# Two-layer decoder trunk: round-trip loads, splits, scores and products issued later, two output chunks interleaved, and some transposes moved from TensorE to VectorE and DMA

## The chip, the cores and the metric

The kernel runs on one core of one Trainium2 chip. The metric is the device time of one execution in microseconds. Before the change it is 958.38 us, the median of three runs (958.22 to 959.68).

## The reference, cut to what matters

`x` is 256 tokens by 2048, in fp32. Layer 0 has eight heads A (a mixture of three dilated windows, computed here as one softmax with counts folded into a mask) and four heads B (differential attention with values of 256). Layer 1 has sixteen causal heads. Both layers have the same shape:

```python
h  = rmsnorm(x, norm) @ w_in                 # 2048 -> 8192 columns: q, k, v and the gate z
ya = softmax(rope(q) rope(k)^T + mask) v     # 24 heads in all
yb = rmsnorm((softmax(q1 k1^T) - lam * softmax(q2 k2^T)) v, subln) * (1 - lam_init)   # heads B
y  = concat(ya, yb) * silu(z)
x  = x + y @ w_out                           # 2048 -> 2048
```

After layer 1 a last rmsnorm follows.

## The kernel before

**Weights set the pace.** Each layer has 20 chunks of 512 weight columns, sixteen of `w_in` and four of `w_out`. A chunk is 16 slots, one for each 128 rows of the weights; the program has 640 slots. In a slot TensorE runs six matmuls of 128x512: two halves of the tokens, and for each three products (`mm3`) of high and low parts, since each fp32 operand is split into two float32r parts whose sum it is. Weights come by DMA (`raw`), ScalarE copies the high part (`wh`, line 123) and VectorE subtracts for the low part (`wl`, line 124), two slots per instruction. The split of slot s is written three such pairs ahead (`AHEAD`), into four buffers.

**Order of chunks.** Layer by layer `v0 q0 k0 z0`, then `q k z v` of groups 1, 2 and 3, then `o0` to `o3` of the output. A group has four heads; groups 2 and 3 of layer 0 have two heads B each, which use two scores per head.

**Work beside the slots** is hung on slots with `at(slot, function)`; it is emitted after the matmuls of that slot. The scheduler below the program may put an instruction earlier on the queue of an engine when it thinks it ready, and engines run their queues in order. With `nxt` for the slot after a chunk's end:

- `evac_rope` (lines 260 to 270, at nxt and nxt+1) turns a chunk of q or k by the rotary tables on VectorE; `evac_z` makes the gate. Both end in `turn`, which brings the token-major 128x512 result into head-dimension-major form: a 32x32-block transpose on VectorE (`bz`, line 240), a store to DRAM (`dt`, line 242) and four loads per half, each of 32 partitions (line 248). All these DMAs are issued by GpSimd's queue, POOL, in its order; each takes it some time, and an issue waits at the head of the queue for what it needs.
- `split_rope` (nxt+18) splits q and k into high and low (`qh`, `kh` on ScalarE, line 279; `ql`, `kl` on VectorE, line 280).
- `first` is nxt of k plus 22 (20 in group 3). `attn_s` for head h at first+3h: scores (`ps_s`) and softmax into `p`. `attn_t` at first+3+3h: transpose of `p` by the same round trip (`bt`, `d`, loads at line 354). `attn_h` at first+15+3h (13 in group 3): splits into `th` (ScalarE, line 363) and `tl` (VectorE). `attn_o` two slots later: the product with v on TensorE (`po`), then `finish_y`, which multiplies by the gate and splits y into `yh`, `yl`.
- Heads B: `diff_s` twice, `attn_t`, `attn_h` at first+15+5h, `diff_o` a slot later (`pdo`; then squares, a power on GpSimd and `yb`), and `diff_y` at first+20+4h: four TensorE transposes of `yb` (line 416) and `finish_y`.
- An output chunk ends in `evac_o` (x plus the product); in layer 0 `next_x` at nxt+3 and nxt+6 makes the next layer's x by eight TensorE transposes per chunk (line 433) and `split_x`.

## Time and profile before

| | |
|---|---|
| median of three runs | 958.38 us |
| the profiled execution | 960.44 us, of which its span on the core 958.7 us |
| TensorE (PE), matmuls | 931.4 us busy, 97% of the span, 4282 instructions |
| VectorE (DVE) | 646.2 us, 67% |
| ScalarE (ACT) | 467.5 us, 49% |
| GpSimd (POOL), DMA issues above all | 214.8 us, 22% |
| DMA engines | 213 MB, 222 GB/s |
| mean granted TensorE clock | 0.991 |

Matmuls overlap, so the duration of one is not what it adds to the path. That is the distance from its start to the start of the next, which the timeline shows. An idle stretch of TensorE stands in brackets before the instruction that ended it, with what released it.

### The profile page before, as it was taken

The numbers are of one execution on the slowest core, as the hardware profiler recorded it, in microseconds if no ns is written. First come the engines' busy times: TensorE is split into PE (matmuls) and PEld (weight loads), VectorE is DVE, ScalarE is ACT, GpSimd is POOL, SyncE is SP. The second block draws the span as 40 slices with busy tenths as digits, with TensorE's granted clock in tenths as the row PEclk, the third lists the DMA queues.
The fourth block names the chain that finished last, engine by engine and source line by source line (L and its number), as shares of the span: only waits on it lengthen the run. The fifth ranks groups of instructions, "written<-read, shape, count | busy, mean of one in ns | idle before, by whom it ended". The sixth has DMA issues, their size and how long they took to land. (4 is left out here: it accounts for less than half of the span.)

```text
span 958.7 us, 11998 instructions
## 1 busy us (share of the span) xinstructions
PE 931.4 (97%) x4282; PEld 773.0 (81%) x4282; DVE 646.2 (67%) x1002; ACT 467.5 (49%) x705; POOL 214.8 (22%) x392
## 2 busy tenths in 40 slices
PE   9999997999999999999999999989999999999996
PEld 7888876888888888878888888768888888887886
DVE  6675876677667767665554667767677767786572
ACT  7533643554355446445454345445534554455450
POOL 0012343242223222200000223522422332251000
PEclk9999998999999999999999999999999999999999
DMA  8785765676666666545555757766666666677542
GB/s 335 257 321 209 248 233 183 237 254 213 230 219 229 215 245 207 196 166 182 194 195 177 249 191 271 239 201 236 237 219 238 247 231 228 220 246 259 179 173 88
DMA packets 43644, 213.22 MB, mean 222 GB/s; under 512 B 9472, under 2 KB 11008, under 8 KB 23488
## 3 DMA queue, kind: packets, MB, share of 16 engines
q1 hardware_dynamic: 27360, 174.55, 52.3%
q0 software_dynamic: 15360, 36.20, 11.4%
q10 hardware_dynamic: 864, 1.70, 0.5%
q8 instruction: 33, 0.54, 0.2%
q14 instruction: 27, 0.22, 0.1%
HBM read 192.23 MB, written 20.19 MB: 222 GB/s over the span
## 5 line engine op out<-in xcount | busy, mean ns | idle before, releaser
L306 PE MATMUL acc<-wh,x 128*128 128x512 f32 x2048 | 645.8, 392 | 0.0
L124 DVE TENSOR_TENSOR wl<-raw,wh 128x1024 fp32r<-128x1024 f32 x314 | 380.0, 1216 | 134.2 <-ACT wh L123 133.0
L306 PEld LDWEIGHTS acc<-wh,x 128*128 128x128 f32 x2048 | 385.7, 188 | 79.0 <-ACT wh L120 0.5
L123 ACT ACTIVATE wh<-raw 128x1024 fp32r<-128x1024 f32 x314 | 328.5, 1055 | 224.3 <-PE acc L306 202.6
L306 PE MATMUL acc<-wl,x 128*128 128x512 f32 x1024 | 400.5, 391 | 2.5 <-DVE wl L124 2.0
L306 PEld LDWEIGHTS acc<-wl,x 128*128 128x128 f32 x1024 | 193.0, 189 | 43.3 <-DVE wl L124 4.6
L306 PE MATMUL acc<-wh,yh 128*128 128x512 f32 x224 | 88.9, 397 | 0.0
L306 PE MATMUL acc<-wl,yh 128*128 128x512 f32 x224 | 88.0, 393 | 0.0
L306 PE MATMUL acc<-wh,yl 128*128 128x512 f32 x224 | 87.9, 393 | 0.0
L242 POOL DMA_DIRECT2D dt<-bz x48 | 27.3, 569 | 264.4 <-DVE bz L240 264.0
L354 POOL DMA_DIRECT2D p<-d x112 | 61.3, 555 | 72.4 <-DMA d<-bt 38.6
L306 PEld LDWEIGHTS acc<-wh,yl 128*128 128x128 f32 x224 | 42.5, 190 | 9.2
L248 POOL DMA_DIRECT2D k<-dt x64 | 34.9, 552 | 66.0 <-DMA dt<-bz 40.2
L306 PEld LDWEIGHTS acc<-wh,yh 128*128 128x128 f32 x224 | 42.5, 190 | 8.7 <-ACT yh L382 0.3
L306 PEld LDWEIGHTS acc<-wl,yh 128*128 128x128 f32 x224 | 42.4, 189 | 8.3
L248 POOL DMA_DIRECT2D u<-dt x64 | 35.0, 553 | 57.0 <-DMA dt<-bz 57.0
L248 POOL DMA_DIRECT2D q<-dt x64 | 35.0, 554 | 55.3 <-DMA dt<-bz 46.2
L320 ACT ACTIVATE p<-p,st 128x128 f32<-128x128 f32 x64 | 28.5, 447 | 33.1 <-DVE st L316 33.1
L280 DVE TENSOR_TENSOR kl<-k,kh 128x512 fp32r<-128x512 f32 x16 | 11.1, 693 | 43.5 <-ACT kh L279 43.5
L279 ACT ACTIVATE kh<-k 128x512 fp32r<-128x512 f32 x16 | 10.1, 632 | 58.2 <-DMA k<-dt 58.2
L363 ACT ACTIVATE th<-p 128x256 fp32r<-128x256 f32 (+1 forms) x28 | 12.0, 428 | 53.8 <-DMA p<-d 51.5
L364 DVE TENSOR_TENSOR tl<-p,th 128x256 fp32r<-128x256 f32 (+1 forms) x28 | 12.3, 439 | 26.8 <-ACT th L363 26.8
(120 smaller groups left out, 656.6 us busy)
## 6 DMA issues: line engine op xcount, KB each, us to landing
raw<-in_w SPq DMA_DIRECT2D x124, 1024.0 KB, 5.2
raw<-in_o SPq DMA_DIRECT2D x32, 1024.0 KB, 4.9
dt<-bz POOLq DMA_DIRECT2D x48, 256.0 KB, 4.1
d<-bt POOLq DMA_DIRECT2D x28, 192.0 KB, 3.4
p<-d POOLq DMA_DIRECT2D x112, 48.0 KB, 3.5
q<-dt POOLq DMA_DIRECT2D x64, 64.0 KB, 4.6
k<-dt POOLq DMA_DIRECT2D x64, 64.0 KB, 3.7
u<-dt POOLq DMA_DIRECT2D x64, 64.0 KB, 4.7
```

What stands on the lines that cost most here:

```text
L123: nc.scalar.activation(ht, r, AF.Copy)
L124: nc.vector.tensor_sub(lt, r, ht.bitcast(F32))
L242: nc.gpsimd.dma_start(d, bt.rearrange("p c h j -> p c (h j)"))
L248: nc.gpsimd.dma_start(t[32 * c:32 * c + 32, i].rearrange("p a h j -> p a (h j)"), box[i][c])
L279: nc.scalar.activation(a, v, AF.Copy)
L280: nc.vector.tensor_sub(b, v, a.bitcast(F32))
L306: nc.tensor.matmul(out_, l, r, start=start and i == 0, stop=stop and i == 2)
L320: nc.scalar.activation(p[:, sl], p[:, sl], AF.Exp, bias=st[:, 0, i:i + 1], scale=-1.0, accum_out=st[:, 1, i:i + 1])
L354: nc.gpsimd.dma_start(pt[32 * c:32 * c + 32], dv[c])
L363: nc.scalar.activation(th4, pt[:, 0:n], AF.Copy)
L364: nc.vector.tensor_sub(tl4, pt[:, 0:n], th4.bitcast(F32))
```

## The change

The program's `turn` loses its loads, which become a function `place` of its own at nxt+8. `split_rope` goes from nxt+18 to nxt+23. `first` becomes nxt+28 (26 in groups 0 and 3). The loads of `p` become `attn_r`, four slots after `attn_t` (three for heads B). `attn_h` comes at first+19+3h (17 in group 3), so scores are 4 to 6 slots later and products with v 8 to 10. The DRAM tiles `d` have four buffers for two.

The output chunks o0 and o1 are cut at 12 of their 16 slots: o0, o1 up to there, then the last four slots of o0 and of o1, then o2 and o3. Weights are laid out in that order on the host. The rows of y that group 3 makes (slots 12 to 15) are thus wanted 12 slots later in o0.

For o0, o1 and o2 of layer 0 the eight TensorE transposes per chunk go: `turn_x` and `place` send the new x through the VectorE and DRAM round trip, and `turned_x` splits it at nxt+19 to nxt+22. The same is done with `yb` for the two heads B of group 2 (`turn` in `diff_o`, `diff_r` for the loads, `diff_y` without TensorE); since `yb` has one buffer, their second head's product comes 19 slots after the first's. 24 and 8 transposes leave TensorE; 8 and 8 stay.

```diff
+def order():
+    return [(i, 0, KT) for i in range(16)] + [(16, 0, 12), (17, 0, 12), (16, 12, KT), (17, 12, KT)] + \
+        [(i, 0, KT) for i in (18, 19)]
...
-    def turn(src, box, name):
-        tt = len(box)
-        bt = work.tile([P, 4, 4, 32], F32, tag="bz", name="bz", bufs=2)
+    def turn(src, box, tt):
+        n = src.shape[1]
+        bt = work.tile([P, n], F32, tag="bz", name="bz", bufs=2).rearrange("p (c h j) -> p c h j", c=4, j=32)
...
-        if tt == 1:
-            box["t"] = t = work.tile([P, 2, 4, 4, 32], F32, tag=name, name=name)
-            for i in range(2):
-                for c in range(4):
-                    nc.gpsimd.dma_start(t[32 * c:32 * c + 32, i].rearrange("p a h j -> p a (h j)"), box[i][c])
+    def place(box, name, *dst, into=None):
+        t = work.tile([P, 2, CW], F32, tag=name, name=name) if into is None else into
+        box["t"] = t = t.rearrange("p t (a h j) -> p t a h j", a=4, j=32)
+        for tt in range(2):
+            for c in range(4):
+                nc.gpsimd.dma_start(t[32 * c:32 * c + 32, tt].rearrange("p a h j -> p a (h j)"), box[tt][c])
...
-        d = dram.tile([P, 4, 3 * 32], F32, tag="d", name="d")
+        d = dram.tile([P, 4, 3 * 32], F32, tag="d", name="d", bufs=4)
...
+    def attn_r(box):
+        pt = box["p"].rearrange("p (a x) -> p a x", a=4)
         for c in range(4):
-            nc.gpsimd.dma_start(pt[32 * c:32 * c + 32], dv[c])
+            nc.gpsimd.dma_start(pt[32 * c:32 * c + 32], box["d"][c])
...
         box["yb"] = yb
+        if g < 3:
+            for tt in range(2):
+                turn(yb[:, tt], box, tt)
+
+    def diff_r(box):
+        place(box, "yb", into=box["yb"])
...
+    def turn_x(n, box, tt):
+        turn(x_sb[:, tt, n * CW:(n + 1) * CW], box, tt)
+
+    def turned_x(n, h, box):
+        kt = 4 * n + h
+        split_x(1, kt, box["t"][:, :, :, h], xhl[kt].rearrange("p b (t a j) -> p b t a j", t=2, a=4))
...
+            at(nxt + 8, place, box, "u" if kind == "z" else kind, layer, g)
             if kind != "z":
-                at(nxt + 18, split_rope, kind, (Q, K)[kind == "k"], layer, g, box)
+                at(nxt + 23, split_rope, kind, (Q, K)[kind == "k"], layer, g, box)
...
-            first = nxt + (20 if late else 22)
+            first = nxt + (26 if g in (0, 3) else 28)
...
-                    at(first + 15 + 5 * h, attn_h, box, True)
-                    at(first + 16 + 5 * h, diff_o, layer, g, h, box)
-                    at(first + 20 + 4 * h, diff_y, layer, g, h, box)
+                    at(first + 8 + 5 * h, attn_r, box)
+                    wait = 5 * h if late else 19 * h
+                    at(first + 18 + wait, attn_h, box, True)
+                    at(first + 19 + wait, diff_o, layer, g, h, box)
+                    if not late:
+                        at(first + 25 + wait, diff_r, box)
+                    at(first + (23 + 4 * h if late else 37 + 19 * h), diff_y, layer, g, h, box)
...
-                    at(first + (13 if late else 15) + 3 * h, attn_h, box)
-                    at(first + (15 if late else 17) + 3 * h, attn_o, layer, g, h, box)
+                    at(first + 7 + 3 * h, attn_r, box)
+                    at(first + (17 if late else 19) + 3 * h, attn_h, box)
+                    at(first + (19 if late else 21) + 3 * h, attn_o, layer, g, h, box)
...
-            if layer == 0:
+            if layer == 0 and g < 3:
+                box = {}
+                for tt in range(2):
+                    at(nxt + 1 + tt, turn_x, g, box, tt)
+                at(nxt + 8, place, box, "qku"[g])
+                for h in range(4):
+                    at(nxt + 19 + h, turned_x, g, h, box)
+            elif layer == 0:
```

POOL's queue at the end of group 0 of layer 0, before: `d` and `p` belong to the round trip of the softmax of one head (stores and loads), `dt` and `q` to that of group 1's q. The rows begin with the store of the third head.

```order
L350 DMA d_1084<-bt_1082 128x384
L354 DMA p_1000<-d_1038 32x4x96 x4
L354 DMA p_1050<-d_1084 32x4x96 x4
L242 DMA dt_1123<-bz_1121 128x512
L350 DMA d_1164<-bt_1162 128x384
L248 DMA q_1141<-dt_1123 32x4x128
L242 DMA dt_1139<-bz_1137 128x512
L248 DMA q_1141<-dt_1123 32x4x128 x3
L248 DMA q_1141<-dt_1139 32x4x128 x4
L354 DMA p_1096<-d_1164 32x4x96 x4
```

The same place of the changed kernel, from the first store of group 1's q:

```order
L248 DMA dt_1093<-bz_1091 128x512
L365 DMA p_1030<-d_1069 32x4x96
L359 DMA d_1135<-bt_1133 128x384
L257 DMA q_1209<-dt_1093 32x4x128
L248 DMA dt_1113<-bz_1111 128x512
L257 DMA q_1209<-dt_1093 32x4x128
L365 DMA p_1077<-d_1135 32x4x96 x3
L359 DMA d_1187<-bt_1185 128x384
L365 DMA p_1077<-d_1135 32x4x96
L257 DMA q_1209<-dt_1093 32x4x128 x2
L257 DMA q_1209<-dt_1113 32x4x128 x4
L365 DMA p_1143<-d_1187 32x4x96 x4
```

The fourth head's loads (the last row of each) stand behind the eight loads of q in both; the other heads' loads now lie among q's stores and loads.

ScalarE's queue at the same place, before, from the split of the third head's `p` (`th_1276`) to that of the fourth (`th_1319`); `qh` is the split of group 1's q, `wh50` serves slots 100 and 101:

```order
L363 ACTIVATE th_1276<-p_1050 128x256
L382 ACTIVATE yh0_607<-y_1223 128x256
L368 ACTIVATE t_1280<-p_1050 128x128
L123 ACTIVATE wh48_1249<-raw24_1202 128x1024
L382 ACTIVATE yh0_607<-y_1266 128x256
L123 ACTIVATE wh49_1282<-raw24_1202 128x1024
L123 ACTIVATE wh50_1307<-raw25_1253 128x1024
L279 ACTIVATE qh_1398<-q_1141 128x512
L382 ACTIVATE yh0_607<-y_1303 128x256
L285 ACTIVATE q_1141<-q_1141 128x512
L123 ACTIVATE wh51_1332<-raw25_1253 128x1024
L363 ACTIVATE th_1319<-p_1096 128x256
```

And of the changed kernel:

```order
L129 ACTIVATE wh51_1296<-raw25_1228 128x1024
L374 ACTIVATE th_1365<-p_1077 128x256
L392 ACTIVATE yh0_598<-y_1291 128x256
L379 ACTIVATE t_1369<-p_1077 128x128
L288 ACTIVATE qh_1420<-q_1209 128x512
L129 ACTIVATE wh52_1338<-raw26_1272 128x1024
L374 ACTIVATE th_1408<-p_1143 128x256
```

`qh` still stands ahead of the fourth head's `th`, one weight split (two slots) later than before; the third head's `th` moved from ahead of `wh48` to behind `wh51`, six slots.

VectorE's queue in group 2 of layer 0, second head B, changed kernel: `yb` from the product, its two transposes, and the two multiplications `y` that read `yb` back after its round trip (before, `y` read TensorE's transpose `ps_yt` one weight split behind `yb`):

```order
L417 SCALAR_TENSOR_TENSOR yb_2976<-pdo_2965,rb_2979,sub_bc_126 128x256 x2
L246 STREAM_TRANSPOSE bz_2985<-yb_2976 128x2x4x32
L130 TENSOR_TENSOR wl118_3016<-raw59_2957,wh118_3015 128x1024
L130 TENSOR_TENSOR wl119_3039<-raw59_2957,wh119_3038 128x1024
L246 STREAM_TRANSPOSE bz_2989<-yb_2976 128x2x4x32
L289 TENSOR_TENSOR kl_3219<-k_3056,kh_3218 128x4x128
L130 TENSOR_TENSOR wl120_3072<-raw60_3019,wh120_3071 128x1024
L130 TENSOR_TENSOR wl121_3090<-raw60_3019,wh121_3089 128x1024
L130 TENSOR_TENSOR wl122_3106<-raw61_3075,wh122_3105 128x1024
L391 SCALAR_TENSOR_TENSOR y_3186<-yb_2976,u_2412 128x256
L391 SCALAR_TENSOR_TENSOR y_3190<-yb_2976,u_2412 128x256
L130 TENSOR_TENSOR wl123_3125<-raw61_3075,wh123_3124 128x1024
```

`wl123`, the split for slots 246 and 247, now stands behind two multiplications that need a DMA to have landed.

## Rows read from the trace of the kernel before

**Rows 1.** The page's first part: busy time and share of the span, TensorE's matmuls (PE) first.

```profile
PE 931.4 (97%) x4282; PEld 773.0 (81%) x4282; DVE 646.2 (67%) x1002; ACT 467.5 (49%) x705; POOL 214.8 (22%) x392
```

**Rows 2.** Stretches in us: length, busy time and instructions of PE, PEld, DVE, ACT and POOL; then the granted clock, the DMA share and GB/s. Two stretches in which TensorE idled in group 0 (layers 0 and 1), one in layer 0's output, one in group 1 of layer 1 and one in the output chunks of layer 0.

```profile
144.00:160.00 16.00, 10.45 (x44) 8.51 (x43) 9.10 (x15) 5.55 (x9) 4.43 (x9) 0.79 0.59 188
396.00:416.00 20.00, 17.34 (x75) 13.33 (x74) 11.19 (x19) 7.59 (x14) 1.66 (x3) 0.91 0.47 163
624.00:640.00 16.00, 11.46 (x47) 9.18 (x46) 12.08 (x19) 6.61 (x10) 3.30 (x6) 0.89 0.47 145
680.00:712.00 32.00, 32.00 (x152) 26.79 (x151) 25.20 (x38) 17.11 (x28) 8.97 (x17) 1.00 0.67 225
432.00:480.00 48.00, 48.00 (x221) 39.73 (x220) 26.90 (x29) 23.85 (x34) 0.00 (x0) 1.00 0.54 192
```

**Rows 3.** The chain of waits in order of time (start, us, what), layer 1: 48 matmuls of 128x512 without anything between, the first product with v of group 1's four heads, and the chunk's matmuls after the fourth.

```profile
675.51 10.89 PE acc L306 x48
686.40 0.35 PE po L306 x3
...
701.06 51.72 PE acc L306 x228
```

**Rows 4.** TensorE's timeline in group 0 of layer 0 (start, us, instruction, count, idle before it and what ended that): the first product of head 0, of head 1, of head 3, and the chunk's first matmul after head 3.

```profile
132.31 0.28 PE L306 MATMUL po<-th,vh 128*128 128x256 f32 x1
...
139.09 0.35 PE L306 MATMUL po<-th,vh 128*128 128x256 f32 x1 [1.33 <-DVE y L381]
...
155.32 0.58 PE L306 MATMUL po<-th,vh 128*128 128x256 f32 x1 [5.55 <-ACT th L363]
...
158.54 0.69 PE L306 MATMUL acc<-wh,x 128*128 128x512 f32 x1
```

**Rows 5.** The same of group 0 of layer 1.

```profile
607.63 0.28 PE L306 MATMUL po<-th,vh 128*128 128x256 f32 x1
...
629.46 0.39 PE L306 MATMUL po<-th,vh 128*128 128x256 f32 x1 [4.54 <-ACT th L363]
...
632.21 0.77 PE L306 MATMUL acc<-wh,x 128*128 128x512 f32 x1
```

**Rows 6.** TensorE's timeline in o0 of layer 0, second head B of group 3: its product, the last matmul before the transposes of `yb`, the transposes, and the chunk's matmul from which on the distances are as elsewhere.

```profile
401.98 0.39 PE L306 MATMUL pdo<-vh,th 128*128 128x256 f32 x1 [0.19 <-ACT th L363]
...
407.40 0.39 PE L306 MATMUL acc<-wh,yl 128*128 128x512 f32 x1
410.17 0.74 PE L416 MATMUL ps_yt<-ident,yb 128*128 128x128 f32 x4 [2.38 <-DVE yb L407]
...
415.10 0.39 PE L306 MATMUL acc<-wh,yh 128*128 128x512 f32 x1
```

**Rows 7.** TensorE's timeline in o0 of layer 1: the matmul ahead of head 3's product of group 3 and the one behind it.

```profile
874.29 0.39 PE L306 MATMUL acc<-wh,yl 128*128 128x512 f32 x1
...
876.11 0.48 PE L306 MATMUL acc<-wh,yh 128*128 128x512 f32 x1
```

**Rows 8.** POOL's timeline in group 0 of layer 0: the store of the fourth head's `p`, loads of q, and the loads of that head's `p`.

```profile
134.42 0.56 POOL L350 DMA_DIRECT2D d<-bt  x1
...
139.47 1.66 POOL L248 DMA_DIRECT2D q<-dt  x3
143.53 2.17 POOL L248 DMA_DIRECT2D q<-dt  x4 [2.40 <-DMA dt<-bz]
145.69 2.18 POOL L354 DMA_DIRECT2D p<-d  x4
```

**Rows 9.** ScalarE's timeline there: the split of q.

```profile
151.31 0.63 ACT L279 ACTIVATE qh<-q 128x512 fp32r<-128x512 f32 x1 [5.99 <-DMA q<-dt]
```

**Rows 10.** VectorE's timeline in o0 of layer 0: the second head's `yb`.

```profile
409.54 0.88 DVE L407 SCALAR_TENSOR_TENSOR yb<-pdo,rb,sub_bc 128x256 f32<-128x256 f32 x2 [0.87 <-POOL rb L189]
```

**Rows 11.** TensorE's timeline around four transposes of the second x in o1 of layer 0; three matmuls of the chunk lie between the second row and the third.

```profile
421.68 0.39 PE L306 MATMUL acc<-wh,yl 128*128 128x512 f32 x1
421.91 0.60 PE L433 MATMUL ps_xt<-ident,x_sb 128*128 128x128 f32 x4
...
423.04 0.40 PE L306 MATMUL acc<-wh,yh 128*128 128x512 f32 x1
```

**Rows 12.** The page's DMA issues: count, KB each and median us from issue to landing.

```profile
dt<-bz POOLq DMA_DIRECT2D x48, 256.0 KB, 4.1
...
p<-d POOLq DMA_DIRECT2D x112, 48.0 KB, 3.5
q<-dt POOLq DMA_DIRECT2D x64, 64.0 KB, 4.6
```

**Rows 13.** VectorE by line and shape: count, busy us and mean ns of one.

```profile
L124 DVE TENSOR_TENSOR wl<-raw,wh 128x1024 fp32r<-128x1024 f32 x314 | 380.0, 1216 | 134.2 <-ACT wh L123 133.0
L266 DVE SCALAR_TENSOR_TENSOR rt<-acc,rn,cosN 128x512 f32<-128x512 f32 x32 | 23.8, 745 | 2.2 <-PE acc L306 2.1
L240 DVE STREAM_TRANSPOSE bz<-rt 128x512 f32<-128x512 f32 x32 | 22.7, 710 | 0.8
L348 DVE STREAM_TRANSPOSE bt<-p 128x384 f32<-128x384 f32 x28 | 16.2, 577 | 9.1 <-DMA d<-bt 8.4
...
L383 DVE TENSOR_TENSOR yl<-y,yh 128x256 fp32r<-128x256 f32 x32 | 13.2, 422 | 14.5 <-ACT yh L382 14.1
```

**Rows 14.** Waits: who waited for what, us in total, times, longest us.

```profile
ACT th L363 <- DMA p<-d: 51.5, 18, 6.5
```

More of the change, by code (lines that the diff above doesn't have):

```diff
@@ L70, in trunk @@
     chunks = [(kind, layer, g) for layer in range(2) for kind, g in layer_chunks()]
-    starts = range(0, KT * len(chunks), KT)
     total = KT * len(chunks)
@@ L148, in trunk, with split_x @@
     x_ins = []
-    def split_x(layer, kt, src):
+    def split_x(layer, kt, src, dst=None):
         g = g_sb[:, layer, kt:kt + 1]
-        h, lo = xhl[kt][:, 0], xhl[kt][:, 1]
+        dst = xhl[kt] if dst is None else dst
+        h, lo = dst[:, 0], dst[:, 1]
         x_ins.append(nc.scalar.activation(h, src, AF.Copy, scale=g).ins)
@@ L255, in evac_z @@
         nc.vector.scalar_tensor_tensor(z, th, 1.0, z, op0=ALU.add, op1=ALU.mult)
-        turn(z, box, "u")
-        if tt == 1:
-            U[layer, g] = box["t"]
+        turn(z, box, tt)
     def evac_rope(ps, name, store, layer, g, tt, box):
@@ L269, in evac_rope @@
         nc.vector.tensor_add(t1, t1, t2)
-        turn(t1, box, name)
+        turn(t1, box, tt)
     def split_rope(name, store, layer, g, box):
@@ L379, in finish_y @@
         y = work.tile([P, S], F32, tag="y", name="y", bufs=2)
-        y4, s4 = (x.rearrange("p (t a j) -> p t a j", t=2, a=4) for x in (y, src))
-        nc.vector.scalar_tensor_tensor(y4, s4, f, u, op0=ALU.mult, op1=ALU.mult)
+        nc.vector.scalar_tensor_tensor(y.rearrange("p (t a j) -> p t a j", t=2, a=4), src, f, u, op0=ALU.mult, op1=ALU.mult)
         nc.scalar.activation(yh[kt], y, AF.Copy)
@@ L390, in attn_o @@
         nc.tensor.matmul(po[:, P:S], v[:, vs], t, start=False, stop=True)
-        finish_y(4 * g + h, po, U[layer, g][:, :, :, h], 0.5)
+        finish_y(4 * g + h, po.rearrange("p (t a j) -> p t a j", t=2, a=4), U[layer, g][:, :, :, h], 0.5)
     def diff_o(layer, g, h, box):
@@ L409, in diff_o @@
         box["yb"] = yb
-    def diff_y(layer, g, h, box):
-        yb = box["yb"]
-        pt = patt.tile([P, 2, S], F32, tag="T", name="ps_yt")
-        for tt in range(2):
-            for d in range(2):
-                nc.tensor.transpose(pt[:, d, tt * P:(tt + 1) * P], yb[:, tt, d * P:(d + 1) * P], ident)
+        if g < 3:
[3 more added lines that the diff above has]
+        place(box, "yb", into=box["yb"])
+    def diff_y(layer, g, h, box):
+        if g == 3:
+            pt = patt.tile([P, 2, S], F32, tag="T", name="ps_yt")
+            for tt in range(2):
+                for d in range(2):
+                    nc.tensor.transpose(pt[:, d, tt * P:(tt + 1) * P], box["yb"][:, tt, d * P:(d + 1) * P], ident)
         for d in range(2):
-            finish_y(4 * g + 2 * h + d, pt[:, d], U[layer, g][:, :, :, 2 * h + d],
-                     0.5 * (1.0 - LAM_INIT))
+            src = pt[:, d].rearrange("p (t a j) -> p t a j", t=2, a=4) if g == 3 else box["t"][:, :, :, d]
+            finish_y(4 * g + 2 * h + d, src, U[layer, g][:, :, :, 2 * h + d], 0.5 * (1.0 - LAM_INIT))
     def evac_o(ps, layer, n):
@@ L512, in trunk @@
     at(L1 + 3, next_sums)
-    for (kind, layer, g), slot0 in list(zip(chunks, starts))[:-1]:
-        ps = pacc.tile([P, 2, CW], F32, tag="acc", name=f"acc{slot0}")
-        nxt = slot0 + KT
+    accs, slot0 = {}, 0
+    for ci, kt0, kt1 in [(20 * layer + i, a, b) for layer in range(2) for i, a, b in order()][:-1]:
+        kind, layer, g = chunks[ci]
+        if kt0 == 0:
+            accs[ci] = pacc.tile([P, 2, CW], F32, tag="acc", name=f"acc{ci}")
+        ps = accs[ci]
+        nxt = slot0 + kt1 - kt0
         for slot in range(slot0, nxt):
@@ L523, in trunk @@
             wh, wl = (x[slot % 2] for x in splits[slot // 2])
-            kt = slot - slot0
+            kt = kt0 + slot - slot0
             for b in range(2):
@@ L531, in trunk @@
                 f(*a)
+        slot0 = nxt
+        if kt1 < KT:
+            continue
         if kind in "zqk":
@@ L568, in trunk @@
             evac_o(ps, layer, g)
-            if layer == 0:
+            if layer == 0 and g < 3:
+                box = {}
+                for tt in range(2):
+                    at(nxt + 1 + tt, turn_x, g, box, tt)
[3 more added lines that the diff above has]
+            elif layer == 0:
                 at(nxt + 3, next_x, g, 0)
@@ L607, in weights @@
         parts = []
-        for kind, g in layer_chunks():
+        for i, kt0, kt1 in order():
+            kind, g = layer_chunks()[i]
             if kind in kinds:
-                c0 = columns(layer, kind, g)
-                parts.append(w[:, c0:c0 + CW].reshape(4, 4, P, CW).transpose(0, 2, 1, 3).reshape(4, P, 4 * CW))
+                c0, n = columns(layer, kind, g), (kt1 - kt0) // 4
+                part = w[kt0 * P:kt1 * P, c0:c0 + CW].reshape(n, 4, P, CW)
+                parts.append(part.transpose(0, 2, 1, 3).reshape(n, P, 4 * CW))
         return np.ascontiguousarray(np.concatenate(parts))
```

11 lines of the change are left out of this document (6 added, 5 removed).

## The prediction

> **What bounds the kernel now.** I read the busy shares first: TensorE's matmuls fill 97% of the span [rows 1], so the time is TensorE's work plus its gaps. I then cut the span into stretches and looked for those in which PE is not full. There are few: around 150 us and 630 us (group 0 of each layer), around 400 us (o0 of layer 0), and a little near 875 us (o0 of layer 1). In the first three the granted clock is below 1 too [rows 2]: after an idle stretch TensorE runs for some us at the lower of its levels, 1.2 instead of 2.4 GHz. Elsewhere PE is full at a clock of 1.00, as in the two other stretches of [rows 2].
>
> Undisturbed TensorE needs 10.89 us for 48 matmuls, so 0.227 us for one and 1.36 us for a slot. Four heads' products with the 54 matmuls between them take 14.66 us, from 686.40 to 701.06 [rows 3]; without the 54 x 0.227 = 12.25 that is 0.60 for a head's product.
>
> - Group 0, layer 0: from the first product at 132.31 to the matmul behind the fourth at 158.54 are 26.23 us [rows 4]. There are 64 matmuls between them (the fourth head is ten later than in group 1), so 14.66 + 10 x 0.227 = 16.93 would do. Lost: **9.3 us**, idle and low clock together.
> - Group 0, layer 1: 632.21 - 607.63 = 24.58 [rows 5], less 16.93: **7.65 us** lost.
> - o0, layer 0: from 407.40 to 415.10 are 7.70 us [rows 6] for 13 matmuls (2.95) and four transposes (0.45, below): **4.3 us** lost.
> - o0, layer 1: 876.11 - 874.29 = 1.82 [rows 7], less 0.23 + 0.60: **1.0 us** lost.
>
> Together 22.25 us. What ends them is a DMA round trip. In group 0 the fourth head's `p` is stored at 134.42, but its loads are issued only at 145.69, behind the eight loads of the next q, which wait at the head of POOL's queue for stores of their own [rows 8]. ScalarE meanwhile stands 5.99 us before the split of that q [rows 9], with `wh`, `yh` and the fourth `th` behind it. In o0 the second head's `yb` is ready at 410.42 (409.54 + 0.88) [rows 10], for a product begun at 401.98 [rows 6]: 8.4 us for a chain to which the code gives four slots.
>
> **The change, part by part.**
>
> *Transposes off TensorE.* Around four of them, 421.68 to 423.04 are 1.36 us for four matmuls, which take 0.91 alone [rows 11]: 0.45 us for a set of four. Six sets of x and two of `yb` go: 8 x 0.45 = **3.6 us**, all on TensorE, thus on the path. The Trainium skill's "VectorE: DVE Perf Modes", section "Rules for kernel authors", speaks against this: a 128x128 transpose belongs on TensorE if PSUM will do as its destination. By that rule the sum would be 3.6 us higher; the rows say that TensorE is the full engine here.
>
> *What takes their place.* For x, six 128x512 transposes of 0.71 us [rows 13], six stores and 24 loads; for `yb` four transposes (an estimate, 0.44 each, from 577 ns at 384 columns and 710 at 512), four stores and 16 loads. VectorE gets 6 us in all. For x this lies in the output chunks, where VectorE is busy 26.9 of 48 us and POOL does nothing [rows 2]; the new x of o2, the last one turned so, is wanted at slot 328, while it is stored at 306 and split at 323. I cost it at nothing. If the cover failed, ScalarE would wait for x as it does for q, at most 6 us once.
>
> *Later loads, splits, scores, products.* Scores are 4 slots later in group 0 and products 8, so the round trip of `p` gets 4 slots, 5.4 us, more; in group 3 it gets 4 slots (heads B: 3 slots, 4.1 us). What TensorE waited was 5.55, 4.54, 2.38 and about 0.5 us [rows 4, 5, 6, 7]. The q of group 1 moves nowhere, so its loads are early enough for the fourth head, whose place in the queue is as bad as before but whose due time is 7 slots (98 to 105), 10 us, later. So I count the 22.25 us as gone. Moving `split_rope` changes little: the scheduler put k's split of group 0 on VectorE's queue behind the same weight split as before.
>
> *Cutting o0 and o1.* No instruction is added, and the loads of weights stay 160. The rows of y of group 3 get 12 slots more and give up 9 or 10 of them to the later products. The PSUM tile of o0 must be emptied within four slots (5.4 us) instead of sixteen; two additions of 128x512, shorter than the 0.745 us of a rotary step of that size [rows 13], take 1.5 us. Cost nothing.
>
> *New waits.* These don't show in the trace, so I bound them.
>
> (a) `yb` of group 2's two heads. Its chain is now: product to `yb` (8.4 us at worst [rows 6, 10]; I take 6, as nothing holds ScalarE for 6 us there), two transposes 0.9, a store 0.6 and its landing 4.1, eight loads at 0.54 [rows 8] 4.4, landing 4.6 as q's [rows 12]: 20.6 us. Foreign stores of q or k stand between them on POOL and wait for a buffer that the small stores hold, another 4.1. So 24.7 us, where the queue of VectorE wants `y` done ahead of the weight split for slot 226 (product at 208) and for 246 (product at 227): 18 and 19 slots, 24.5 and 25.9 us, less 2 us for `y` and the split. So it is late by 2.2 and 0.8 us by this sum, early by 2 and 3 without the foreign stores; the ends are 0 and 6.5 us each, the longest wait for `p` [rows 14]. Nothing below 0, since no TensorE work hangs on it. I take 1 us each, near the lower end as TensorE's own gap is shorter than its helpers'. **+2.**
>
> (b) `yb` of group 3: three slots stay between the second product and its transposes, 4.1 us, plus the product itself. Between 0 and 4.3 us; with ScalarE no longer late I take **+0.5.**
>
> (c) Group 0's products in both layers: between 0 and 5.55 each [rows 4]; the due time moved by 10 us against 9.3 lost, so I take **+0.5** each.
>
> (d) In the middle groups the products now lie on the rotary work of the next q (slots 144 and 145, products at 146 to 155). I take **+0.5** for all; the other end is a rival, below.
>
> Sum: -22.25 - 3.6 + 4.0 = -21.85 us. The profiled span of 958.7 becomes 936.9, the profiled execution 960.44 becomes 938.6; that one is 2.1 above the median, and the median of 958.38 becomes **936.5 us**.
>
> **Rivals.**
>
> 1. *No new wait.* Then only the gains count: 958.4 - 25.9 = 932.5, and with some small waits for `wl` gone as well 931. For it: (a) misses by little and (b) to (d) are guesses upward. Against it: TensorE's helpers wait 51.5 us for `p` alone [rows 14], and 20 DMAs are added next to them. The Trainium skill, "DMA: Bandwidth & Descriptors", section "Anatomy of one DMA — SWDGE (gpsimd) path", gives about 2.0 us plus bytes over 436 GB/s, an estimate of 2.15 us for a load of 64 KB. By it every round trip would be short enough and this rival would hold; the trace has 4.6 us for that load.
>
> 2. *POOL's block stays.* The fourth head's loads still stand behind q's eight. If q's stores come as late as now, group 0 loses its 16.95 us again, and only 4.3 + 1.0 + 3.6 are gained, less 2 us of (a): 951.5. With half of it gone 943. For it: the unchanged queue. Against it: the fourth product is 7 slots later, and q's stores were late because the products' work lay on VectorE between them; it now comes after them.
>
> 3. *The collision moves* (slower). In group 0 the next q is turned while products are due, and this costs 9.3 us; in group 1 of layer 0 and groups 1 and 2 of layer 1 that was not so and now is. VectorE has from slot 144 to the third head's product at 152 eight slots and two products, 12.1 us. In it lie two rotary halves (0.745 and 0.71, and three steps between half and full width, 0.4 to 0.7 each: about 3.1 us, so 6.2 [rows 13]), three weight splits of 1.22, two `y` and two `yl` of 0.42, one `tl`: 6.2 + 3.6 + 1.7 + 0.4 = 11.9 us. It decides from where that sum exceeds 12.1 us plus the lead of about two slots: three places at 9.3 us, 27.9 against the 21.85 gained, give 964.5. Against it: the first two `tl` stand ahead of the rotary work in VectorE's queue, and the lead is 2.7 us.
>
> 4. *The change doesn't do what it says*, because the scheduler hoists loads and splits to where they were, and TensorE's gaps stay: 958.4 - 3.6 + 4 = 958.8. Against it: scores and products stand 4 to 10 slots later on TensorE's queue in every group.
>
> **How the numbers follow.** Forecast (932 to 941) 0.57; rival 1 (below 932) 0.17; rival 2 (941 to 952) 0.17; rival 3 0.06; rival 4 0.03. The predicted time is 936.5 us. The lower end of the range is that of rival 1 with small gaps gone, 929; the upper reaches through the half of rival 2 that lies near 943, to 946. Out are the other part of rival 2 and rivals 3 and 4, 0.17, and 0.03 below. A run here tells 0.2%, 1.9 us, from no change: faster 0.92, same 0.02, slower 0.06.
>
> **What would show it.** Right: in the stretches of group 0 PE full and the granted clock 1.00; no idle time of over 1 us before a product with v; `ps_xt` with 8 transposes and `ps_yt` with 8; VectorE about 6 us busier, POOL about 27 us (50 more issues); TensorE's gaps mostly before matmuls that wait for `wl`, around slots 226 and 246. Wrong: idle time before the fourth product again, with POOL's loads of q ahead of `p` (rival 2); waits for `tl` or `wl` in groups 1 and 2 at the end of the next q's chunk (rival 3); `x` waiting for its loads at the start of layer 1. What I may have mis-sized most is (a): its terms come from rows of other round trips, and each wait long enough lowers the clock behind it.

## The result, and the profile after

The changed kernel takes **946.16 us** (median of four runs, 944.32 to 947.83) against 959.03 for the kernel before on the same chip. The ratio is 0.9864, 95% interval 0.9822 to 0.9905: 12.9 us faster, between 9 and 17. The forecast was 936.5, so the direction was right and the gain some 9 us smaller. The upper end of the range, 946 of a time before of 958.38, is a ratio of 0.9871; the measured one lies just inside it. The profiled execution took 944.32 us, its span is 942.5.

The busy shares, against [rows 1]:

```profile
PE 921.6 (98%) x4250; PEld 767.3 (81%) x4250; DVE 648.1 (69%) x1012; ACT 466.7 (50%) x705; POOL 241.4 (26%) x442
```

TensorE runs 32 instructions fewer, the transposes, and is 9.8 us less busy. GpSimd has 50 DMA issues and 26.6 us more, as forecast (27). VectorE is only 1.9 us busier where 6 were forecast, although its ten new transposes fill 5.6 us (six of x 4.0, four of `yb` 1.6); what became shorter in exchange I did not trace.

Stretches (columns as in [rows 2]): group 0 of layer 0, o0 of layer 0, group 0 of layer 1, and two stretches that were not on the list before.

```profile
144.00:160.00 16.00, 14.26 (x69) 11.47 (x68) 12.78 (x23) 7.24 (x13) 5.49 (x10) 1.00 0.63 193
396.00:416.00 20.00, 20.00 (x102) 16.91 (x101) 12.34 (x21) 9.28 (x18) 1.39 (x2) 1.00 0.45 158
600.00:616.00 16.00, 16.00 (x77) 13.40 (x76) 11.39 (x18) 8.21 (x13) 6.89 (x13) 1.00 0.88 308
440.00:448.00 8.00, 7.02 (x30) 5.25 (x30) 5.17 (x7) 4.62 (x8) 1.12 (x3) 1.00 0.34 105
464.00:480.00 16.00, 13.23 (x53) 10.16 (x52) 7.04 (x12) 7.12 (x13) 1.76 (x4) 0.89 0.43 140
```

o0 and group 0 of layer 1, where PE had been busy 17.34 of 20 us and 11.46 of 16, are now full, at a clock of 1.00. Group 0 of layer 0 is nearly full. The two last rows are new holes: o2 of layer 0, and the start of layer 1, where the clock also falls.

TensorE's timeline in group 0 of layer 0, against [rows 4]: the first head's product, the third's, the fourth's and the matmul behind it.

```profile
143.29 0.28 PE L315 MATMUL po<-th,vh 128*128 128x256 f32 x1
...
153.36 0.35 PE L315 MATMUL po<-th,vh 128*128 128x256 f32 x1 [0.52 <-DVE y L391]
...
158.12 0.28 PE L315 MATMUL po<-th,vh 128*128 128x256 f32 x1
159.62 0.39 PE L315 MATMUL po<-tl,vh 128*128 128x256 f32 x1 [1.22 <-DVE tl L375]
...
160.10 0.48 PE L315 MATMUL acc<-wh,x 128*128 128x512 f32 x1
```

From 143.29 to 160.10 are 16.81 us. All heads now stand three slots apart, so the undisturbed 14.66 us of [rows 3] apply: 2.15 us are lost in place of 9.3.

TensorE's timeline at the two new holes:

```profile
443.61 0.49 PE L315 MATMUL acc<-wh,yh 128*128 128x512 f32 x1 [0.21 <-ACT wh L129]
444.87 0.50 PE L315 MATMUL acc<-wl,yh 128*128 128x512 f32 x1 [0.77 <-DVE wl L130]
...
474.14 0.49 PE L315 MATMUL acc<-wh,x 128*128 128x512 f32 x1 [2.01 <-ACT wh L129]
475.40 0.50 PE L315 MATMUL acc<-wl,x 128*128 128x512 f32 x1 [0.77 <-DVE wl L130]
475.74 0.66 PE L315 MATMUL acc<-wh,x 128*128 128x512 f32 x2
476.21 0.62 PE L315 MATMUL acc<-wl,x 128*128 128x512 f32 x1
476.63 1.05 PE L315 MATMUL acc<-wh,x 128*128 128x512 f32 x2
```

The idle time is small, but TensorE waits for weights that ScalarE has not split (first for those of slot 302, then of slot 322), and after the second hole one matmul takes 0.42 us (from 476.21 to 476.63) in place of 0.23: the lower clock. ScalarE's timeline says why the splits were late:

```profile
441.70 0.91 ACT L160 ACTIVATE x<-q,g_sb 128x256 fp32r<-128x256 f32 x2 [8.08 <-DMA k<-dt]
...
471.44 1.71 ACT L160 ACTIVATE x<-u,g_sb 128x256 fp32r<-128x256 f32 x4 [9.08 <-DMA u<-dt]
```

ScalarE stood 8.08 and 9.08 us at the head of its queue before the split of the new x of o0 (its tile is `q`) and of o2 (tile `u`), with `wh` behind it. The first row's releaser is named as a load of `k`, which is x of o1; what that split reads is x of o0, whose last two loads were issued from 434.75 on; the semaphore of the later one has its last event at 441.46, just before the split. The loads were issued late, on POOL's timeline:

```profile
434.75 1.09 POOL L257 DMA_DIRECT2D q<-dt  x2 [1.75 <-DMA q<-dt]
...
455.12 1.14 POOL L248 DMA_DIRECT2D dt<-bz  x2 [10.03 <-DVE bz L246]
460.95 4.36 POOL L257 DMA_DIRECT2D u<-dt  x8 [4.69 <-DMA dt<-bz]
```

For o2 POOL waits 4.69 us for its own store to land, then needs 4.36 us to issue eight loads; the last is issued at 464.8 and x arrives 6.6 us later.

The end of the program hides the third surprise. Every engine runs an instruction DRAIN there. Those of POOL and SyncE (count, ns shortest/median/longest, first and last start), before and after, each kernel in a fence of its own:

```profile
L634 POOLq DRAIN  x3: 40/102/5753, 952.1 to 958.4; - x3
L634 SPq DRAIN  x3: 7/7/7, 957.8 to 958.1; - x3
```

```profile
L680 POOLq DRAIN  x3: 40/102/9833, 931.9 to 942.3; - x3
L680 SPq DRAIN  x3: 7/7/7, 937.7 to 942.0; - x3
```

POOL's first DRAIN begins right after the last work, 952.1 before and 931.9 after, so TensorE's path is **20.2 us** shorter. But it takes 5.75 us before, which ends level with SyncE's wait for the stores of the output (its DRAIN begins at 957.8), and 9.83 us after, to 941.7, 4 us longer than that wait (937.7). The program ends 4 us later than its output. So 20.2 less 4.0 is the 16.2 us by which the span fell.

### The profile page after: what moved, and what is told of

The parts are those of the page before. It is cut to its first block, busy times and chain, and to the rows that moved or that the text cites. A ratio compares the mean times of both kernels' runs of the same rounds, so it can differ in the third digit from the quotient of the medians.

```text
span 942.5 us, 12025 instructions
## 1 busy us (share of the span) xinstructions
PE 921.6 (98%) x4250; PEld 767.3 (81%) x4250; DVE 648.1 (69%) x1012; ACT 466.7 (50%) x705; POOL 241.4 (26%) x442
## 4 chain that ended last, share of the span: by engine, by line
PE 76%; DMA 10%; issue 6%; POOL 3%; DVE 2%; ACT 1%; SPq 0%; POOLq 0%; DVEq 0%; ACTq 0%
PE acc L315 72%; DMA dt<-bz 3%; DMA q<-dt 3%; DMA d<-bt 2%; PE last L492 1%; DMA p<-d 1%; PE ps_s L315 1%; DMA raw<-in_w 1%; PE po L315 1%; ACT wh L129 1%; POOL q L257 1%; DMA u<-dt 1%; POOL u L257 1%; DVE wl L130 1%; PE ps_s L320 1%
## 5 line engine op out<-in xcount | busy, mean ns | idle before, releaser
L248 POOL DMA_DIRECT2D dt<-bz x58 | 32.8, 566 | 239.7 <-DVE bz L246 239.3
L257 POOL DMA_DIRECT2D k<-dt x72 | 39.3, 551 | 65.8 <-DMA dt<-bz 32.6
L257 POOL DMA_DIRECT2D u<-dt x72 | 39.2, 551 | 64.1 <-DMA dt<-bz 60.1
L257 POOL DMA_DIRECT2D q<-dt x72 | 39.2, 551 | 59.2 <-DMA dt<-bz 37.4
L374 ACT ACTIVATE th<-p 128x256 fp32r<-128x256 f32 (+1 forms) x28 | 12.0, 428 | 33.5 <-DMA p<-d 31.6
L275 DVE SCALAR_TENSOR_TENSOR rt<-acc,rn,cosN 128x512 f32<-128x512 f32 x32 | 23.8, 742 | 2.8 <-PE acc L315 2.7
```

The costliest lines, as they stand in the source:

```text
L248: nc.gpsimd.dma_start(d, bt.rearrange("p c h j -> p c (h j)"))
L257: nc.gpsimd.dma_start(t[32 * c:32 * c + 32, tt].rearrange("p a h j -> p a (h j)"), box[tt][c])
L275: nc.vector.scalar_tensor_tensor(a4, p4, r, co, op0=ALU.mult, op1=ALU.mult)
L374: nc.scalar.activation(th4, pt[:, 0:n], AF.Copy)
```

## The experiments

Measured times are medians; ratios are to the kernel before on the same chip and of means, so they need not be the quotient of two medians. Executions of one kernel scatter over 10 us and more (before: 947.27 to 961.07 in 25), so an interval is some 0.35% to each side, 3.3 us, and smaller effects are read from the traces.

**The changed kernel again.**

> The changed kernel itself, unedited, as the measure for the others on this chip and as a second look at its waits. Theory: the waits for x near slots 302 and 322 belong to the kernel and come again (1.4 and 5.2 us of PE in its first trace, each between 1 and 5 us here); the products of the second layer's group 0 (slots 422 and 425), which lost 0.45 us in its first trace but 3.6 to 5.3 us in the traces of three kernels that do not differ there, lose some us here too: their wait depends on how long the transfers of p take to land and moves from execution to execution. Rival: those products wait only where the edits of those three kernels made them, and lose under 0.5 us here. The last DRAIN of GpSimd takes 9.83 us again.

Measured: 947.16 us, ratio 0.9897 (0.9866 to 0.9928). The waits for x came again, smaller: ScalarE 7.2 and 7.6 us, TensorE idle 0.40 us at slot 302 and 0.88 + 0.76 at slot 322. Slots 422 and 425 lost nothing here, as the rival says, but the rival does not hold: the kernel with 12 small transfers (below) has none of those edits and lost 2.0 us there. Group 0 of layer 0 lost 4.2 us (143.75 to 162.60, less 14.66) in place of 2.15, so the size does move from execution to execution. The DRAIN took 9.833 us, the same to a nanosecond. VectorE waits for `yb`, as in the first trace (4.47 us, which TensorE did not feel there), but longer, and now TensorE waits too:

```profile
363.27 0.76 DVE L391 SCALAR_TENSOR_TENSOR y<-yb,u 128x256 f32<-128x256 f32 x2 [5.95 <-DMA yb<-dt]
```

```profile
365.22 0.50 PE L315 MATMUL acc<-wl,x 128*128 128x512 f32 x1 [0.93 <-DVE wl L130]
...
368.83 0.50 PE L315 MATMUL acc<-wl,x 128*128 128x512 f32 x1 [0.59 <-DVE wl L130]
```

These are slots 246 and 248: term (a) at one of the two slots that the prediction named.

**x of o0 to o2 back on TensorE, and of o2 alone** (there with `g < 2` in place of `False`).

```diff
-            if layer == 0 and g < 3:
+            if False:
```

> The changed kernel with one part undone: the second x of o0, o1 and o2 is turned by TensorE again, as that of o3 is; all else stays. Theory: in the changed kernel ScalarE stands before the splits of x of o1 and o2 (8.08 and 9.08 us in the trace) because x comes back late from DRAM, and TensorE loses about 1.4 us near 443 us and about 5.2 us near 472 to 476 us for it. Both losses should be gone; the 24 transposes cost 6 sets of 0.45 = 2.7 us. GpSimd issues 30 transfers fewer (400 in place of 430), and if its last DRAIN goes by their number (9.83 us with 430, 5.75 us with 380: 0.082 us each) it shrinks to about 7.4 us. Sum: 946.2 - 6.6 + 2.7 - 2.4 = about 940. Rival: the two losses come from something else at the start of the second layer (weights late, the clock) and stay: then the transposes alone count, 946.2 + 2.7 = 949, less what the DRAIN gives, 946.5. A third reading, that the DRAIN has nothing to do with the number of transfers: 942.3 if the waits are gone.

> The changed kernel with the second x of o2 alone turned by TensorE again (o0 and o1 keep the way through DRAM). Theory: the loss of about 5.2 us near 472 to 476 us is that of o2's x and goes; 8 transposes cost 0.9 us; the DRAIN (420 transfers) gives 0.8 us: 946.2 - 5.2 + 0.9 - 0.8 = about 941. The loss near 443 us stays. Rival (the loss has another cause): 946.2 + 0.9 - 0.8 = 946.3.

Measured: 948.0 (0.9917, 0.9886 to 0.9948) and 945.74 (0.9905, 0.9870 to 0.9940). With all three x on TensorE the holes are gone and the clock is full, in the stretches that had them:

```profile
440.00:448.00 8.00, 8.00 (x37) 6.64 (x36) 3.45 (x4) 3.18 (x3) 0.00 (x0) 1.00 0.46 146
464.00:480.00 16.00, 16.00 (x75) 13.24 (x74) 8.91 (x11) 8.06 (x11) 0.69 (x1) 1.00 0.55 199
```

With o2's x alone put back, the hole at slot 322 is gone and that at slot 302, which belongs to o0's x, stays (0.77 us idle), as expected; but TensorE now waits 0.27 and 1.11 us before o2's transposes, the second time for VectorE's split of the set before:

```profile
461.68 0.63 PE L457 MATMUL ps_xt<-ident,x_sb 128*128 128x128 f32 x4 [1.11 <-DVE x L161]
```

The cause of the holes is thus x's way through DRAM, and the DRAIN took 7.38 and 9.02 us as expected. But neither time is told apart from the changed kernel's; the expected 940 and 941 were not reached. In both traces group 0 lost more than in the first trace of the changed kernel: the third head's product waited 2.01 and 2.09 us in layer 0, 1.53 and 3.43 in layer 1.

**yb of group 2 back on TensorE.**

```diff
-        if g < 3:
+        if False:
             for tt in range(2):
                 turn(yb[:, tt], box, tt)
...
-        if g == 3:
+        if True:
...
-                    if not late:
+                    if False:
                         at(first + 25 + wait, diff_r, box)
```

> The changed kernel with yb of group 2 of the first layer turned by TensorE again, at the slots that the changed kernel gives it. Theory: the way of yb through DRAM is covered there, so undoing it gives back nothing on the path and costs 2 sets of 0.45 = 0.9 us, and the DRAIN (410 transfers) gives 1.6 us: about 945.5. Rival (prediction's term a, a hidden wait for yb of 2 us or more): 943.5 or less. If the DRAIN does not go by the number of transfers: 947.1.

Measured: 950.17 (0.9969, 0.9936 to 1.0001), some 5 us slower than expected. Its trace (945.9 us, the shortest of its twelve executions) has no wait at slots 246 and 248, and its DRAIN took 8.20 us; what made the other executions longer it does not show. It has the holes of x and loses 3.8 us in group 0 of layer 1. The next kernel undoes the same and more and is not slower, so I draw no price from this one.

**All transposes back on TensorE** (both edits above).

> The changed kernel with all transposes back on TensorE (the second x of o0 to o2 and yb of group 2): the later loads, splits, scores and products and the interleaving alone are left. Theory: 8 sets of 0.45 = 3.6 us come back on TensorE; the waits for x near slots 302 and 322 (4.8 to 6.4 us in two traces of the changed kernel) go; GpSimd issues 380 transfers as before the change, so its last DRAIN takes 5.75 in place of 9.83 us and the end comes 4.1 us earlier: 946.5 + 3.6 - 5 - 4.1 = about 941. So the part of the change that takes transposes off TensorE would be a loss of some 5 us here. Rival: the waits for x have another cause and the products of group 0 wait as much: 946.5 + 3.6 - 4.1 = 946.

Measured: 947.68 (0.9881, 0.9837 to 0.9925), no different from the changed kernel. Holes at 440 and 464 us gone; DRAIN 5.752 us with 380 transfers, as before the change; in exchange 3.6 us of transposes and, in this trace, 4.4 and 2.7 us lost in group 0 of the two layers and 3.23 us idle before a product in o0 of layer 1:

```profile
877.41 0.36 PE L315 MATMUL po<-th,vh 128*128 128x256 f32 x1 [3.23 <-DVE y L391]
```

So the later slots and the interleaving alone give the gain, and taking transposes off TensorE is worth nothing that can be measured here; the intervals, some 0.4% to each side, are about as wide as the 3.6 us in question. It was expected to be a loss of 5 us, which also is not seen (two of the six executions, 939.86 and 940.97 us, lie there, the other four from 947.67 to 949.04).

**Loads early, products late** (`place` at nxt+1, `attn_r` with `attn_t`, for heads B too, where it also stood four slots behind), **and loads late, products early.** The second puts the splits of q and k, the scores and the products of the heads A back at their slots of before; `attn_o` moves with `attn_h`.

```diff
-            at(nxt + 8, place, box, "u" if kind == "z" else kind, layer, g)
+            at(nxt + 1, place, box, "u" if kind == "z" else kind, layer, g)
...
-                    at(first + 7 + 3 * h, attn_r, box)
+                    at(first + 3 + 3 * h, attn_r, box)
```

```diff
-                at(nxt + 23, split_rope, kind, (Q, K)[kind == "k"], layer, g, box)
+                at(nxt + (23 if layer == 0 and g >= 2 else 18), split_rope, kind, (Q, K)[kind == "k"], layer, g, box)
...
+                first = nxt + (20 if late else 22)
...
-                    at(first + (17 if late else 19) + 3 * h, attn_h, box)
+                    at(first + (13 if late else 15) + 3 * h, attn_h, box)
```

> The changed kernel with the placing loads of q, k, u and p written right behind their stores again, as in the kernel before; all scores, splits and products stay at the changed kernel's slots. Theory: with the products later the block on GpSimd's queue is covered, and the time is within 2 us of the changed kernel's. Rival: the block on GpSimd's queue itself is what the change removed, and 5 us or more come back in the groups 0.

> The changed kernel with the scores, the splits of q and k and the products with v of the groups without subtraction (the first layer's 0 and 1, the second layer's all) back at the slots of the kernel before; the placing loads stay in rows of their own, 4 slots behind the stores. Theory: the later products are what covers p's way through DRAM, and without them the waits of group 0 come back at both places: 5 to 9 us in each layer as against 2 to 5 in the changed kernel, so 5 to 10 us over it. Rival: separating the loads from the stores did it alone, and the time is within 2 us of the changed kernel's.

Measured: 948.62 (0.9912, 0.9879 to 0.9944) with the loads early, within 1.5 us of the changed kernel on the same chip. With the products early 971.09 (1.0139, 1.0101 to 1.0176): 24 us over the changed kernel and 13 over the kernel before. So the later splits, scores and products carry the gain; which of the three, and whether the four buffers of `d` (in all these kernels) have a share, was not tried apart. The 13 us over the kernel before fit the later loads, though this kernel also has the interleaving and the moved transposes: `th` waits for `p` longer, against [rows 14] and against 31.6 us in 15 times in the changed kernel:

```profile
ACT th L374 <- DMA p<-d: 68.1, 16, 9.1
```

The harm is larger than the 5 to 10 us expected. In this trace a part of it lies at slot 176, where ScalarE stands 11.85 us before the split of group 2's k (7.09 in the changed kernel) and TensorE waits for weights behind it:

```profile
272.31 0.80 PE L315 MATMUL acc<-wh,x 128*128 128x512 f32 x1 [3.69 <-ACT wh L129]
```

**Plain order of the output chunks** (with group 3 at its old slots, which plain order needs).

```diff
-    return [(i, 0, KT) for i in range(16)] + [(16, 0, 12), (17, 0, 12), (16, 12, KT), (17, 12, KT)] + \
-        [(i, 0, KT) for i in (18, 19)]
+    return [(i, 0, KT) for i in range(20)]
```

> The changed kernel with the chunks of the output in plain order again (o0 whole, then o1), and, since o0 then needs group 3's rows of y at its slot 12, with the splits, scores and products of group 3 back at the slots of the kernel before; all else stays. Theory: the waits at the end of o0's first rows come back, 4.3 us in the first layer and 1.0 in the second, and the time is 4 to 7 us over the changed kernel's 946 to 947, so 951 to 953. Rival: the interleaving only pays for group 3's later slots, and with both undone the time is within 2 us of the changed kernel's.

Measured: 958.23 (1.0008, 0.9980 to 1.0036): all of the gain gone, 11 us, more than the 4 to 7 expected, and elsewhere than expected. The wait for `yb` in o0 of layer 0 did not come back; TensorE waits earlier, for the split of group 3's k, and in layer 1 for the product's helpers:

```profile
366.80 0.38 PE L314 MATMUL ps_s<-kh,qh 128*128 128x256 f32 x1 [1.21 <-ACT kh L287]
368.32 0.58 PE L314 MATMUL ps_s<-kl,qh 128*128 128x256 f32 x1 [1.14 <-DVE kl L288]
...
868.36 0.36 PE L314 MATMUL po<-th,vh 128*128 128x256 f32 x1 [3.05 <-DVE y L390]
```

So undoing the interleaving with the slots that it gives to group 3 takes away the whole gain, as undoing the later slots of the heads A did. How much of the 11 us is the order and how much group 3's slots was not tried apart. Not all of it is in these waits: group 0 of layer 0, which the edit leaves alone, lost 7.2 us in this trace.

**Products of group 0 six slots later still.**

```diff
-                    at(first + (17 if late else 19) + 3 * h, attn_h, box)
+                    at(first + (17 if late else 25 if g == 0 else 19) + 3 * h, attn_h, box)
```

> The changed kernel with the products with v of the groups 0 (their splits of p and the products, both layers) 6 slots later still; all else stays. Theory: what is left of the wait for p in group 0 (2.7 to 8.7 us in the first layer, 0.3 to 5.3 in the second, in the traces of the kernels that do not differ there) is p's way through DRAM outlasting the cover, and 6 slots (8 us) more cover it: 3 to 8 us less, about 941 to 942, and under 0.5 us lost at slots 96 to 112 and 400 to 432. Rival: the loads of p stand behind the placing of q on GpSimd's queue, so something that follows (the splits of q and k of group 1, or the stores) is late next and takes the place of the wait: within 2 us of the changed kernel.

Measured: 946.92 (0.9899, 0.9862 to 0.9936), no gain. The rival held for layer 0: TensorE stands 2.09 us before the second head's product, and VectorE and ScalarE show what is late next:

```profile
158.64 0.39 PE L315 MATMUL po<-th,vh 128*128 128x256 f32 x1 [2.09 <-DVE y L391]
```

```profile
151.23 0.63 ACT L288 ACTIVATE qh<-q 128x512 fp32r<-128x512 f32 x1 [6.43 <-DMA q<-dt]
```

```profile
151.90 0.69 DVE L289 TENSOR_TENSOR ql<-q,qh 128x512 fp32r<-128x512 f32 x1 [5.44 <-ACT qh L288]
```

The split of the next q waits for its loads, as in [rows 9] (5.99 us), and holds both helpers for some 6 us. The changed kernel has that wait too, shorter:

```profile
149.44 0.63 ACT L288 ACTIVATE qh<-q 128x512 fp32r<-128x512 f32 x1 [3.76 <-DMA q<-dt]
```

That the backlog behind it is what TensorE then waits for is my reading of the order of these rows; no kernel with an earlier or later split of q was tried.

**What the DRAIN goes by.** 100 and 12 transfers of 32 bytes are added; the edit is that of the first kernel, the second has 12 single ones that read `ssq`:

```diff
+    for i in range(20):
+        at(L1 + 100 + 4 * i, tiny, 5)
```

> The changed kernel plus 100 transfers of 32 bytes each from SBUF to a scratch place in DRAM, issued by GpSimd in the second layer (5 at every fourth slot from the hundredth of the layer on); nothing reads them. Theory: GpSimd's last DRAIN goes by the number of transfers that it issued: 9.83 + 100 x 0.082 = about 18 us, the span and the time 8 us longer, about 954; the waits of TensorE stay as they are. Rival: the DRAIN goes by bytes or packets moved (17312 packets in the queue, 1952 more than before the change): 100 packets more give 0.2 us, about 946.4. Second rival: the DRAIN goes by neither: 946.2.

> The changed kernel plus 12 transfers of 32 bytes from SBUF to a scratch place in DRAM, issued by GpSimd after the last chunk of the first layer (near 480 us, where it has nothing else to issue); nothing reads them. The last DRAIN took 5.75, 7.38, 8.20, 9.02 and 9.83 us with 380, 400, 410, 420 and 430 transfers, 0.082 us for each, but 7.55 us with 530, which is what 402 would give: 128 fewer. Theory: the DRAIN goes by the transfers issued since the last of some count of 128; as 430 stands at 120.5 steps of 0.082 us if nothing else is in it, 442 is past the next turn and its DRAIN takes about 0.4 us. Then the end is set by the stores of the output, which were done 4.0 us before the end in the changed kernel's trace: about 4 us less than the kernel without the 12. Rival: the 530's smaller value comes from where or how its 100 transfers were issued (they ran in the first 350 us), not from a turn: then 9.83 + 12 x 0.082 = 10.8 us and a time 1 us longer.

Measured: 968.95 (1.0149, 1.0115 to 1.0183) with 100; the scheduler issued them from 31 us on, not in layer 1, and they held up POOL's round trips in the first groups, so that time says nothing on the DRAIN, which took 7.55 us: the simple count (18 us) is wrong, and so is that of packets (3200 more in the queue, not the 100 that the expectation took; 2.1 ns each as between 380 and 430 transfers would make it 16.5 us). With 12 the DRAIN took **1.34 us**:

```profile
L686 POOLq DRAIN  x3: 40/102/1340, 938.1 to 944.4; - x3
L686 SPq DRAIN  x3: 7/7/7, 943.8 to 944.1; - x3
```

SyncE's wait for the output ends last again, at 943.8. The stretch behind the start of POOL's DRAIN is 4.0 us shorter than in the changed kernel (944.7 - 938.1 against 942.5 - 931.9). The time, 944.68 (0.9863, 0.9826 to 0.9901), is 2.5 us under the changed kernel's on the same chip, which the intervals do not tell from none. In the two traces of that chip the spans are equal, 944.7: POOL's DRAIN begins 4.0 us later here (938.1 against 934.1), since group 0 lost 8.3 us in layer 0 (143.86 to 166.86, less 14.66) and 2.0 in layer 1. The small transfers were issued from 484 to 492 us, so they did not cause the first of these losses.

**The three edits together** (o2's x on TensorE, group 0's products later, 12 transfers).

> Three edits on the changed kernel together: the second x of o2 back on TensorE, the products of the groups 0 six slots later, and 12 transfers of 32 bytes more on GpSimd after the last chunk of the first layer. Theory: about 3 us less for o2's x (its wait of 3 to 5 us against 0.9 of transposes), 3 to 8 us less in the groups 0, and 4 us less at the end (GpSimd's last DRAIN took 1.34 us with the 12): 946.5 - 3 - 5 - 4 = about 934.5, faster than both kernels. Rival: the waits of group 0 do not go (see the kernel with the products later alone), and o2's x leaves o1's wait larger: 940 to 943.

Measured: 945.37 (0.9891, 0.9847 to 0.9934). Not the expected 934.5: group 0 of layer 0 still waits (2.20 us before a product), slots 246 and 248 too, o2's transposes wait 1.10 us for a split of x, and the DRAIN took 9.18 us where 1.34 or less was hoped for. No version was found that is measurably faster than the changed kernel.

## Why the prediction came out as it did

By terms of its sum, in the two profiled executions (forecast -21.85, span -16.2):

- *Group 0, 9.3 and 7.65 us gone, and term (c), +0.5 each.* Layer 1: right, nothing lost in the two traces of the changed kernel, though 2.0 with the 12 small transfers and 2.7 to 4.9 where x or yb was put back. Layer 0: mis-sized. 2.15 us are left in the first trace and about twice that in the second; the eight traces in which this group's slots are those of the changed kernel and POOL was not held up lost 0.2 to 8.3 us. The step "early enough for the fourth head" missed that the split of the next q keeps a wait and the helpers with it (by the reading above); that is the smaller half of rival 2.
- *o0, 4.3 and 1.0 us gone.* Right in layer 0: PE is full from 396 to 416 us. In layer 1 0.37 us of idle time stayed. The plain order shows that the slots given to group 3 also spare other waits, which the prediction did not price.
- *Transposes, 3.6 us.* Right as a price on TensorE, but not as a gain: see the next step. The Trainium skill's "VectorE: DVE Perf Modes", section "Rules for kernel authors", would have left them on TensorE. The kernel with all of them back is not measurably slower (0.9881 against 0.9897), so no harm of the rule is seen here, against my reading that the full engine decides.
- *"What takes their place: at nothing".* **This step failed.** The price for a failed cover was named, at most 6 us once, and x waiting for its loads at the start of layer 1 stood among the signs of being wrong. ScalarE waited 8.08 and 9.08 us, and TensorE lost 1.4 us (0.21 + 0.77 idle and slower matmuls) and about 5 us (2.01 + 0.77 idle, the rest at the lower clock). I had counted from the slot where x of o2 is wanted (328) and its split emitted (323). The scheduler put the split earlier, ahead of weight splits that TensorE wanted at slot 322, so its due time was theirs; the split of o0's x, emitted from slot 303 on, stood ahead of weights wanted at 302.
- *(a), +2 us.* Right in kind and place: nothing in the first trace, where VectorE's wait for `yb` is hidden, and 0.93 + 0.59 us at slots 246 and 248 in the second. (b): nothing seen. (d): nothing seen between 640 and 840 us.
- *The end of the program* had no term. It costs 4.0 us, through the 50 added transfers.

By these terms TensorE's path would have fallen by 22.25 + 3.6 - 2.15 - 0.4 - 6.4 = 16.9 us. It fell by 20.2; the other 3.3 are small gaps elsewhere, no single one of a microsecond, which I don't assign. So on TensorE the sum was nearly right in part by luck, by terms that were not, and the end made most of the difference in the span. The time lies in the interval that rival 2 had, but only the 2 to 4 us of group 0 are of its mechanism. Rival 1 fell. The Trainium skill's "DMA: Bandwidth & Descriptors", section "Anatomy of one DMA — SWDGE (gpsimd) path", by which a load of 64 KB is an estimate of 2.15 us, is far from this trace, where the medians even rose for q, from 4.6 [rows 12]; the page's DMA issues after the change:

```profile
dt<-bz POOLq DMA_DIRECT2D x54, 256.0 KB, 4.1
d<-bt POOLq DMA_DIRECT2D x28, 192.0 KB, 4.2
p<-d POOLq DMA_DIRECT2D x112, 48.0 KB, 4.3
q<-dt POOLq DMA_DIRECT2D x72, 64.0 KB, 5.1
k<-dt POOLq DMA_DIRECT2D x72, 64.0 KB, 3.7
u<-dt POOLq DMA_DIRECT2D x72, 64.0 KB, 5.8
```

Rivals 3 and 4 fell too: no wait moved into the middle groups, and the gaps in o0 and in layer 1 went.

Open: why yb alone on TensorE is slower than with x as well, and what sets the size of group 0's wait in one execution.

## What to carry to other kernels

Time a step that goes through DRAM against what stands behind it on its engine's queue, not against its own consumer; a scheduler may have put it ahead of work that is due sooner. Distance between producer and consumer carried the gain here (taking it away cost 11 us in one place and 24 in the others, where the loads stayed late); moving work to an idle engine gave nothing measurable, since waits for that work came in its place. Read the last DRAINs of a trace as part of the path.

## What the runs showed of the hardware that was not expected

Without added small transfers, GpSimd's final DRAIN lengthens with the number of transfers that GpSimd issued in the program:

| transfers issued by GpSimd | kernels | longest DRAIN, us |
|---|---|---|
| 380 | before; all transposes back | 5.753; 5.752 |
| 400 | x on TensorE | 7.383 |
| 410 | yb on TensorE | 8.202 |
| 420 | x of o2 on TensorE | 9.018 |
| 430 | changed (twice), plain order; products later, loads early, products early | 9.833; 9.835 |
| 430 + 12 small | | 1.340 |
| 420 + 12 small | the three edits | 9.180 |
| 430 + 100 small | | 7.547 |

Up to 430 that is 0.0816 us for each (4.08 us for 50), on a line to within 0.01 us. With small transfers added it falls back by an amount that these three kernels do not settle: 100 of them give what 402 would (128 fewer than 530), but 12 gave two different drops. That the count alone does not set it is shown; the rule is open. At 380 the DRAIN ends level with the wait for the stores of the output (no kernel here issued fewer), and from there to 430 each transfer costs its 0.08 us at the end.
